# A list scheduler's price for a GpSimd step, and the place of a reload in the DMA queue

## The chip, the cores and the metric

The kernel runs on one core of a Trainium2 chip. The metric is device time in microseconds (us) of one execution, the median of several runs. A second figure, the span, runs from the first to the last instruction of one profiled execution.

## The reference

One mixer layer over 2048 positions of width 1024, all in float32. Two groups of heads share one input projection; what matters here is group B, gated DeltaNet with 8 heads of width 128 in chunks of 64 positions:

```python
xn = rmsnorm(h, norm_w[i]);  proj = einsum('bsd,de->bse', xn, w_in[i])
...
A = where(strict, einsum('bhnik,bhnjk->bhnij', k_beta, k) * L, 0.0)
T = triangular_solve(A + eye, eye, left_side=True, lower=True, unit_diagonal=True)
u = einsum('bhnij,bhnjv->bhniv', T, v * beta[..., None])
w = einsum('bhnij,bhnjk->bhnik', T, k_beta * exp(decay)[..., None])
...
def step(state, inp):                       # scan over the chunks of a head
    v_new = u_c - w_c @ state
    o_c = q_c @ state + qk_c @ v_new
    state = state * a_c + k_c.T @ v_new
```

So each chunk needs a 64x64 unit lower triangular system solved, and each head then needs a recurrence over its chunks. Group A (a gated MLP over blocks of 128 positions), the output projection, a gate with an embedding of its own and a last RMSNorm follow in the same program.

## The kernel before

**Passes and units.** The 2048 positions are worked through in two passes of 1024. In each pass TensorE first does four units of the projection for group A (`v_unit`), then for each of the 8 heads three units: `kq_unit` (keys and queries), `vu_unit` (values), `zz_unit` (gates). A unit is four projections of 24 matmuls each (`proj`, two halves `b` of 512 positions by two blocks of columns). After both passes come the output projection (`out_stream`, PSUM tile `pso`) and the gate (`pg`).

**The order of the work.** The kernel writes its instructions in an order that a list scheduler (`class Flow`, L31) makes while the program is built. Its clock `fl.t` advances by a price for each matmul; `fl.clk` holds a clock for VectorE, ScalarE and GpSimd, advanced by a price for each instruction (`act` L134, `tt` L147, `gtt` L178, `asel` L182, `power` L174 and others). The stream of projections runs until a gate is shut; tasks (`fl.spawn`) wake at the times that they name and put their instructions between the matmuls of the stream. On the chip each engine then executes its instructions strictly in the written order and waits at semaphores. All DMAs are issued by the SP queue, in the written order as well. So a price in `Flow` is not a time on the chip; it decides which instruction stands before which.

**A head's path.** `front` (L719) makes the 64x64 systems of one half of a head in `AT` and writes them to DRAM (`atd`, L780). When both halves are written, `inverse` (L811) solves the 16 systems of the head on GpSimd: it loads `xs` (the identity, from `xinit`, L815) and pieces of `atd` (`ain`, two buffers, L822), waits 4500 ns of the scheduler's time, and then does 63 columns, each with two `gtt` instructions, a product into `xtmp` (L833) and a subtraction from `xs` (L835). At the end it writes `xs` to DRAM (`td`, L841), waits 2600 ns, waits for the chain of the head before (`done`), loads the two diagonal halves of `Dt` (L848) and spawns `chain`. `chain` (L851) is the recurrence: eight steps, each a row of small matmuls into `pc` and `po` with VectorE and ScalarE work between; the second matmul of a step needs `Dt`. Four steps make a half; then the buffer of keys and queries of that half (`kq`) is given back at L907, and `finish` (L919) takes a power on GpSimd (`sso`) and writes `ysc`.

**Gates that matter.** `inverse` of a head starts when its systems are written and when `inverted` has an entry for the head before (L812). `kq_unit` needs one of four `kq` buffers for each half (L672); each head holds two until its chain has given them back, so half `b` of head h+2 waits for half `b` of the chain of head h. At the end of each pass `refill` (L970) stages the next stationary operands through `kq`, `acc` and `pre` buffers too.

Of the kernel before, what the change touches and what calls it, by code (L numbers as in the profile page):

```python
# [106 lines left out]
def trunk(tc, a, out):  # L107
# [7 lines left out]
    fl = Flow()  # L115

    def width(ap):
        return int(np.prod(ap.shape[1:]))

    def mm(o, lhsT, rhs, start, stop):  # L120
        nc.tensor.matmul(o, lhsT, rhs, start=start, stop=stop)  # L121
        n = width(rhs)
        fl.t += max(109.0, 4 + 0.4453 * n) if lhsT.dtype == F32R else max(222.0, 1.7 * n)
        return fl.t + 220
# [9 lines left out]
    def act(o, i, func, after=None, **kw):  # L134
        nc.scalar.activation(o, i, func, **kw)  # L135
        c = 60 + 0.85 * width(i) + (93 if "accum_out" in kw else 0)
        if local(i):
            c += 35
        if not isinstance(kw.get("scale", 1.0), float):
            c += 100  # L140
        t = TABLES.get(func)
        if t and t != fl.table:
            fl.table = t
            c += 1290
        return fl.op("act", c, after)

    def tt(o, x, y, op, after=None):  # L147
        nc.vector.tensor_tensor(o, x, y, op)  # L148
        return fl.op("dve", 76 + 1.04 * width(o), after, local(x, y))

    def stt(o, x, sc, y, op0, op1, after=None):
        nc.vector.scalar_tensor_tensor(o, x, sc, y, op0, op1)  # L152
        return fl.op("dve", (76 if isinstance(sc, float) else 135) + 1.04 * width(o), after, local(x, y))

    def ts(o, x, s1, s2, op0, op1=None, after=None):
        if op1 is None:
            nc.vector.tensor_scalar(o, x, s1, s2, op0)
        else:
            nc.vector.tensor_scalar(o, x, s1, s2, op0, op1)  # L159
        w = width(o)  # L160
        c = 70 + 0.7 * w
        if not isinstance(s1, float):
            c = 135 + (2.6 if op1 is not None else 1.04) * w
        return fl.op("dve", c, after, local(x))
# [12 lines left out]

    def gtt(o, x, y, op, after=None):  # L178
        nc.gpsimd.tensor_tensor(o, x, y, op)  # L179
        return fl.op("pool", 330 + 1.6 * width(o), after)  # L180

    def asel(o, x, after=None):  # L182
        nc.gpsimd.affine_select(o, x, [[0, 4], [1, P]], ALU.is_ge, 0.0, 0, -1)
# [2 lines left out]
    with ExitStack() as outer:  # L186
# [12 lines left out]
        def bank(tag, name, shape=(P, 4, P)):  # L199
            return pp.tile(list(shape), F32, tag=tag, bufs=2 if tag in ("pj", "tr", "m") else 1, name=name)  # L200
# [29 lines left out]
        def gt(tag, name, shape, bufs, dt=F32):  # L230
            return gp.tile(list(shape), dt, tag=tag, bufs=bufs, name=name)
# [487 lines left out]
        def front(p, h, b, st):  # L719
# [64 lines left out]
            if b == 1:  # L784
                fl.spawn(inverse(p, h, st), 2500, 1)
# [25 lines left out]
        def inverse(p, h, st):  # L811
            while 2 * len(inverted) < st["i"]:  # L812
                yield fl.t + 300
            xs = gt("xs", "xs", [P, 8, 64], 1)
            dma(xs, a["xinit"])  # L815
            tmp = gt("xtmp", "xtmp", [P, 160], 1)
            asys = st["atd"].rearrange("b u d j i -> (b u d) (j i)")
            ains = {}

            def load(jc):  # L820
                ains[jc] = gt("ain", "ain", [P, 8, 64], 2)
                dma(ains[jc].rearrange("p j i -> p (j i)"),  # L822
                    asys[None, :, jc * 512:(jc + 1) * 512].to_broadcast([8, 16, 512]))
            load(0)
            load(1)
            yield fl.t + 4500
            for j in range(63):
                if j % 2 == 0:
                    yield from fl.room("pool", 500)
                jc, jj = divmod(j, 8)  # L830
                n, kk = 63 - j, j // 8 + 1
                t_ = tmp[:, :kk * n].rearrange("p (k n) -> p k n", k=kk)
                gtt(t_, ains[jc][:, jj, None, j + 1:].to_broadcast([P, kk, n]),  # L833
                    xs[:, :kk, j:j + 1].to_broadcast([P, kk, n]), ALU.mult)
                f = gtt(xs[:, :kk, j + 1:], xs[:, :kk, j + 1:], t_, ALU.subtract)  # L835
                if jj == 7 and jc < 6:
                    yield f
                    load(jc + 2)
            yield f
            td = dp.tile([64, 16, 64], F32, tag="td", bufs=2, name="td")  # L840
            dma(td.rearrange("(k c) s i -> (c s) k i", c=8), xs)  # L841
            inverted.append(1)
            yield fl.t + 2600
            while len(done) < st["i"]:
                yield fl.t + 300
            for d in range(2):
                dd = slice(d * 64, d * 64 + 64)
                dma(Dt[dd, :, dd], td.rearrange("c (u d) i -> d c u i", d=2)[d])  # L848
            fl.spawn(chain(p, h, st), 4500, 0)

        def chain(p, h, st):  # L851
            beta, gh, gl, ex, ne = SC[p]
            while len(done) < st["i"] or len(st["R"]) < 2:
                yield fl.t + 300
            Sp = state[:, h, :]
            outs = []
            for b in range(2):
                kq, kd, vn, AT, QK, bn, qe = st["B"][b]
                yield from fl.take("ot")
                ot = gt("ot", "ot", [P, 4, P], 1)  # L860
                sso = gt("sso", "sso", [P, 4], 2)
                for u in range(4):
                    c = h * 8 + b * 4 + u
                    cu = slice(c, c + 1)
                    first = p + b + u == 0
                    last = b == 1 and u == 3
                    pc = bank("ch", "pc")
                    if first:
                        r = vn[:, u]
                    else:  # L870
                        yield mm(pc[:, 0], kq[:, u, 0, :], Sp, True, True)
                        r = gt("r", "r", [P, P], 1)
                        yield stt(r, pc[:, 0], ne[:, cu], vn[:, u], ALU.mult, ALU.add)
                    f = mm(pc[:, 1], Dt[:, b * 4 + u], r, True, True)
                    while outs[-1:] == [0]:
                        yield fl.t + 100
                    po = bank("o", "po", [P, 2, P])
                    if not first:
                        mm(po[:, 0], kq[:, u, 1, :], Sp, True, True)
                    yield f  # L880
                    yield act(x1[0:64], pc[0:64, 1], AF.Copy)
                    f = mm(pc[:, 2], AT[:, u], x1, True, True)
                    if not first:
                        act(ot[:, u], po[:, 0], AF.Copy, scale=ex[:, 0, cu])
                    yield f
                    yield tt(r[64:128], r[64:128], pc[64:128, 2], ALU.subtract)
                    yield mm(pc[:, 1], Dt[:, b * 4 + u], r, True, True)
                    w = gt("w", "w", [P, P], 1)
                    yield ts(w, pc[:, 1], bn[:, u:u + 1], None, ALU.mult)
                    more = not (last and p == NPASS - 1)  # L890
                    if more:
                        f = mm(pc[:, 3], kd[:, u], w, True, True)
                    fo = mm(po[:, 1], QK[:, u], w, True, True)
                    outs.append(0)
                    fl.spawn(gather(ot[:, u], po[:, 1], sso[:, u:u + 1], first, outs), fo - fl.t, 0)
                    if more:
                        yield f
                        Sn = state[:, h, :] if last else gt("S", "S", [P, P], 2)
                        if first:
                            f = vcopy(Sn, pc[:, 3])  # L900
                        else:
                            f = stt(Sn, Sp, ex[:, 2, cu], pc[:, 3], ALU.mult, ALU.add)
                        Sp = Sn
                        yield f
                while outs[-1] == 0:
                    yield fl.t + 100
                fl.give("kq")  # L907
                fl.spawn(finish(p, h, b, st, ot, sso, qe, outs[-1]), 0, 1)

        def gather(o, po, ss, first, outs):  # L910
            i = len(outs) - 1
            if first:
                yield vcopy(o, po)
            else:
                yield tt(o, o, po, ALU.add)
            junk = gt("junk", "junkc", [P, P], 2, BF16)
            outs[i] = act(junk, o, AF.Square, accum_out=ss)
# [349 lines left out]
        done, fronts, inverted, SC, mixed, stored, vdone, prepped, Ls = [[] for _ in range(9)]  # L1267
# [114 lines left out]
```

## Time and profile before

| what | value |
|---|---|
| median of 3 runs | 2332.24 us (2331.82 to 2336.56) |
| the profiled execution, its own time | 2334.43 us |
| its span | 2332.7 us |
| mean granted TensorE clock over the span | 0.985 of full |
| busy share: TensorE, VectorE, GpSimd, ScalarE | 96%, 55%, 49%, 43% |

The busy shares are means over the span; GpSimd has little to do outside the two passes of heads. The profiled execution is 2.2 us above the median, and 1.7 us of its time lies outside the span.

### The profile page before, as it was taken

To read this page: it belongs to the slowest core of one execution; us is meant where nothing else is said; L and a number is where in the kernel's file an instruction comes from. 1 tells how busy PE (TensorE), PEld (TensorE's weight loads), DVE (VectorE), ACT (ScalarE), POOL (GpSimd) and SP (SyncE) were. 2 spreads that over 40 slices of the span, in tenths; PEclk is the share of its full clock that TensorE was granted. 3 is DMA by queue.
4 is the path that set the end of the run, shared out by engine and by line. 5 is a ranking of instruction groups with operands and counts; after the bars stand their busy time and mean duration, and the time that the engine had idled before them with its cause. 6 is when DMAs were issued, how large, how long until landed. Compare 5 with 4: busy or idle time off the path is not lost.

```text
span 2332.7 us, 34766 instructions
## 1 busy us (share of the span) xinstructions
PE 2250.4 (96%) x11884; PEld 1878.9 (81%) x11884; DVE 1293.3 (55%) x2845; ACT 999.1 (43%) x2398; POOL 1131.6 (49%) x2246
## 2 busy tenths in 40 slices
PE   8999899999999999999899999999989999999998
PEld 8988688787787779987788878778778878878886
DVE  5465375574665755347466566575664243346665
ACT  5554354453444443445345454454432232244443
POOL 1118668586686772137768668668660000001111
PEclk9999999999999999999999999999999999999999
DMA  5632232323222243222332332232453466452221
GB/s 185 228 117 88 73 99 79 98 72 101 89 87 80 79 148 114 77 76 80 89 98 80 96 99 78 87 87 85 126 167 121 150 200 194 139 185 74 79 77 63
DMA packets 249201, 253.22 MB, mean 109 GB/s; under 512 B 66112, under 2 KB 163904, under 8 KB 249024
## 3 DMA queue, kind: packets, MB, share of 16 engines
q1 hardware_dynamic: 249024, 251.01, 34.6%
q8 instruction: 93, 1.52, 0.3%
q14 instruction: 84, 0.69, 0.1%
HBM read 195.89 MB, written 55.05 MB: 108 GB/s over the span
## 4 chain that ended last, share of the span: by engine, by line
PE 78%; POOL 11%; DMA 5%; issue 2%; DVE 2%; ACT 1%; SPq 1%; POOLq 0%; DVEq 0%; ACTq 0%
PE pj L121 36%; PE pso L121 13%; PE pg L121 7%; PE pc L121 6%; PE pv L121 6%; POOL xs L179 5%; POOL xtmp L179 4%; DMA Dt<-td 2%; PE po L121 2%; PE pe L121 2%; PE pkq L121 1%; DMA wo<-in_wo 1%; DMA td<-xs 1%; PE pm L121 1%; PE ph L127 1%
## 5 line engine op out<-in xcount | busy, mean ns | idle before, releaser
L179 POOL TENSOR_TENSOR xtmp<-ain,xs 128x132 f32<-128x132 f32 (+47 forms) x1008 | 462.4, 459 | 250.9 <-DMA ain<-atd 180.4
L179 POOL TENSOR_TENSOR xs<-xs,xtmp 128x132 f32<-128x132 f32 (+47 forms) x1008 | 483.2, 479 | 79.0
L175 POOL TENSOR_TENSOR rstd<-rstd,nhalf 128x1 f32<-128x1 f32 x64 | 45.8, 722 | 577.3 <-DVE rstd L159 290.3
L121 PE MATMUL pj<-xlo,whi 128*128 128x512 f32 x768 | 315.3, 411 | 0.0
L121 PE MATMUL pj<-xhi,wlo 128*128 128x512 f32 x768 | 314.9, 410 | 0.0
L121 PE MATMUL pj<-xhi,whi 128*128 128x512 f32 x768 | 314.2, 409 | 0.0
L121 PE MATMUL pj<-xrhi,whi 128*128 128x512 f32 x768 | 313.2, 408 | 0.0
L121 PE MATMUL pj<-xrhi,wlo 128*128 128x512 f32 x768 | 312.3, 407 | 0.0
L121 PE MATMUL pj<-xrlo,whi 128*128 128x512 f32 x768 | 311.0, 405 | 0.0
L152 DVE SCALAR_TENSOR_TENSOR acc<-pre,cw,acc 128x512 f32<-128x512 f32 x288 | 227.8, 791 | 23.9 <-ACT acc L135 19.4
L121 PE MATMUL pso<-wolo,yhi 128*128 128x512 f32 x512 | 204.9, 400 | 2.3 <-DVE wolo L148 2.2
L121 PE MATMUL pso<-wohi,ylo 128*128 128x512 f32 x512 | 205.3, 401 | 0.0
L121 PE MATMUL pso<-wohi,yhi 128*128 128x512 f32 x512 | 202.5, 395 | 0.0
L148 DVE TENSOR_TENSOR wlo<-raw,whi 128x512 fp32r<-128x512 f32 x224 | 163.9, 734 | 62.5 <-ACT whi L135 61.6
L135 ACT ACTIVATE whi<-raw 128x512 fp32r<-128x512 f32 x224 | 140.3, 629 | 95.2 <-PE pj L121 71.0
L135 ACT ACTIVATE yhi<-yraw 128x512 fp32r<-128x512 f32 x128 | 80.3, 630 | 215.3 <-PE pso L121 208.6
L121 PEld LDWEIGHTS pj<-xlo,whi 128*128 128x128 f32 x768 | 147.2, 192 | 24.3
L121 PEld LDWEIGHTS pj<-xhi,wlo 128*128 128x128 f32 x768 | 147.0, 191 | 23.9
L121 PEld LDWEIGHTS pj<-xhi,whi 128*128 128x128 f32 x768 | 146.9, 191 | 23.7
L121 PEld LDWEIGHTS pj<-xrhi,wlo 128*128 128x128 f32 x768 | 145.7, 190 | 25.1
L121 PEld LDWEIGHTS pj<-xrlo,whi 128*128 128x128 f32 x768 | 146.0, 190 | 24.5
L148 DVE TENSOR_TENSOR ylo<-yraw,yhi 128x512 fp32r<-128x512 f32 x128 | 89.5, 701 | 135.9 <-ACT yhi L135 133.2
(202 smaller groups left out, 4858.3 us busy)
## 6 DMA issues: line engine op xcount, KB each, us to landing
raw<-in_wu SPq DMA_DIRECT2D x224, 256.0 KB
ain<-atd SPq DMA_DIRECT2D x128, 256.0 KB
yraw<-ysc SPq DMA_DIRECT2D x128, 256.0 KB
vsc<-gv SPq DMA_DIRECT2D x64, 128.0 KB
gn<-vsc SPq DMA_DIRECT2D x32, 256.0 KB
ysc<-gn SPq DMA_DIRECT2D x32, 256.0 KB
ysc<-zb SPq DMA_DIRECT2D x32, 256.0 KB
wo<-in_wo SPq DMA_DIRECT2D x32, 256.0 KB
```

The source lines that it names most:

```text
L121: nc.tensor.matmul(o, lhsT, rhs, start=start, stop=stop)
L127: nc.tensor.transpose(o, i, ident)
L135: nc.scalar.activation(o, i, func, **kw)
L148: nc.vector.tensor_tensor(o, x, y, op)
L152: nc.vector.scalar_tensor_tensor(o, x, sc, y, op0, op1)
L175: nc.gpsimd.tensor_tensor(o, x, y, ALU.pow)
L179: nc.gpsimd.tensor_tensor(o, x, y, op)
```

## The change

Three numbers of the scheduler and the place of one line change. The price of a `gtt` instruction rises from 330 + 1.6 ns per column to 375 + 1.95 ns per column. The entry in `inverted`, which lets the next head's `inverse` issue its loads of `xs` and `ain`, is made after the two loads of `Dt` are issued, no longer right after the write of `td`. The chain is spawned 5000 ns after the loads of `Dt` in place of 4500. No instruction is added or removed; their order changes.

```diff
     def gtt(o, x, y, op, after=None):
         nc.gpsimd.tensor_tensor(o, x, y, op)
-        return fl.op("pool", 330 + 1.6 * width(o), after)
+        return fl.op("pool", 375 + 1.95 * width(o), after)
...
             dma(td.rearrange("(k c) s i -> (c s) k i", c=8), xs)
-            inverted.append(1)
             yield fl.t + 2600
             while len(done) < st["i"]:
                 yield fl.t + 300
             for d in range(2):
                 dd = slice(d * 64, d * 64 + 64)
                 dma(Dt[dd, :, dd], td.rearrange("c (u d) i -> d c u i", d=2)[d])
-            fl.spawn(chain(p, h, st), 4500, 0)
+            inverted.append(1)
+            fl.spawn(chain(p, h, st), 5000, 0)
```

## Rows read from the trace of the kernel before

**Rows 1.** The page, its first part: busy us (share) x instructions of each engine.

```profile
PE 2250.4 (96%) x11884; PEld 1878.9 (81%) x11884; DVE 1293.3 (55%) x2845; ACT 999.1 (43%) x2398; POOL 1131.6 (49%) x2246
```

**Rows 2.** Waits of TensorE over the span: total us, times, longest us.

```profile
PE pc L121 <- DMA Dt<-td: 53.7, 15, 9.5
```

**Rows 3.** The same view, stretches 1100 to 1130 and 1460 to 1500.

```profile
PE pc L121 <- DMA Dt<-td: 8.1, 1, 8.1
...
PE pc L121 <- DMA Dt<-td: 2.2, 1, 2.2
```

**Rows 4.** GpSimd by line, 1378 to 1470: busy us, mean ns | idle before, releaser.

```profile
L179 POOL TENSOR_TENSOR xs<-xs,xtmp 128x56 f32<-128x56 f32 (+47 forms) x63 | 30.1, 478 | 4.9
L179 POOL TENSOR_TENSOR xtmp<-ain,xs 128x56 f32<-128x56 f32 (+47 forms) x63 | 29.1, 463 | 14.7 <-DMA ain<-atd 10.3
L175 POOL TENSOR_TENSOR sso<-sso,nhalf 128x4 f32<-128x4 f32 x2 | 2.1, 1058 | 4.1 <-DVE pre L167 2.2 <-DVE sso L152 1.9
```

**Rows 5.** Timeline of GpSimd: start us, duration us, the instruction [idle before, releaser].

```profile
1383.86 0.29 POOL L179 TENSOR_TENSOR xtmp<-ain,xs 128x63 f32<-128x63 f32 x1 [10.33 <-DMA ain<-atd]
...
1475.07 0.29 POOL L179 TENSOR_TENSOR xtmp<-ain,xs 128x63 f32<-128x63 f32 x1 [10.15 <-DMA ain<-atd]
```

**Rows 6.** Timeline of the SP queue, two heads: start us, us of issuing.

```profile
1101.78 0.38 SPq L841 DMA_DIRECT2D td<-xs  x1
1104.36 0.33 SPq L815 DMA_DIRECT2D xs<-in_xinit  x1
...
1106.22 1.23 SPq L848 DMA_DIRECT2D Dt<-td  x2
...
1463.98 0.38 SPq L841 DMA_DIRECT2D td<-xs  x1
1466.62 1.22 SPq L848 DMA_DIRECT2D Dt<-td  x2
...
1469.24 0.59 SPq L815 DMA_DIRECT2D xs<-in_xinit  x1
1470.75 1.27 SPq L822 DMA_DIRECT2D ain<-atd  x2
```

**Rows 7.** The chain that ended last, the same two heads: start us, us, what.

```profile
1106.82 7.32 DMA Dt<-td
...
1467.21 2.91 DMA Dt<-td
```

**Rows 8.** Timeline of ScalarE: end of a chain, then query half 0 of a later head.

```profile
306.13 0.31 ACT L135 ACTIVATE junkc<-ot 128x128 bf16<-128x128 f32 x1 [2.61 <-DVE ot L148]
308.90 0.58 ACT L135 ACTIVATE pre<-pj 128x512 f32<-128x512 f32 x1
...
390.25 0.31 ACT L135 ACTIVATE junkc<-ot 128x128 bf16<-128x128 f32 x1 [3.45 <-DVE ot L148]
399.79 0.60 ACT L135 ACTIVATE pre<-pj 128x512 f32<-128x512 f32 x1 [0.63 <-PE pj L121]
...
583.13 0.30 ACT L135 ACTIVATE junkc<-ot 128x128 bf16<-128x128 f32 x1
587.25 0.60 ACT L135 ACTIVATE pre<-pj 128x512 f32<-128x512 f32 x1 [0.79 <-PE pj L121]
...
1164.25 0.31 ACT L135 ACTIVATE junkc<-ot 128x128 bf16<-128x128 f32 x1
1166.45 0.60 ACT L135 ACTIVATE pre<-pj 128x512 f32<-128x512 f32 x1 [1.28 <-PE pj L121]
...
1428.82 0.31 ACT L135 ACTIVATE junkc<-ot 128x128 bf16<-128x128 f32 x1 [4.51 <-DVE ot L148]
1436.39 0.60 ACT L135 ACTIVATE pre<-pj 128x512 f32<-128x512 f32 x1 [0.42 <-PE pj L121]
```

**Rows 9.** Stretches: length, busy us (x) of PE, PEld, DVE, ACT, POOL; clock; DMA.

```profile
258.00:262.00 4.00, 4.00 (x13) 3.33 (x12) 1.45 (x4) 0.75 (x2) 3.37 (x9) 0.50 0.14 36
...
1113.50:1117.00 3.50, 2.73 (x10) 2.47 (x11) 0.21 (x1) 0.64 (x2) 2.87 (x9) 0.50 1.08 345
```

## The prediction

> **What bounds the kernel now.** I read the page first. TensorE is busy 96% of the span, 2250.4 of 2332.7 us [rows 1], so what a change of order can win is bounded by the 82 us in which TensorE is idle, and by what its clock loses. The view of waits names the owner of that time: 53.7 us in 15 waits is one thing, a chain matmul that waits for `Dt` [rows 2]. The reader is to see that 15 of the 16 heads pay, that the longest pays 9.5 us, and that it differs by place: an early head of a pass pays 8.1, a settled one 2.2 [rows 3].
>
> Why is `Dt` late? The groups of GpSimd by line and its timeline answer, over one settled head. The 63 products and 63 subtractions are busy 30.1 + 29.1 us, with small gaps of 4.9 + (14.7 - 10.3) us between them: 68.5 us [rows 4]. The scheduler's old price for the same 126 steps is 126 x 330 ns + 1.6 ns x 12,768 columns = 62.0 us (12,768 is twice the sum over the 63 columns of (j//8 + 1)(63 - j)). So the scheduler believes that the inverse ends 6.5 us before it does, writes the chain's matmuls too early into TensorE's order, and TensorE, which executes in order, stands there.
>
> The last view is the SP queue. In a settled head `Dt` is already issued ahead of the next head's `xs` and `ain`; only at the first head of the pass does `xs` go first [rows 6]. There `Dt` shares the DMA engines with those loads, and the chain shows it landing after 7.32 us where a settled head takes 2.91 [rows 7].
>
> **The price of a step.** The new price is 126 x 375 ns + 1.95 ns x 12,768 = 72.1 us: 10.1 us above the old one and 3.6 us above the 68.5 measured. With 500 ns more before the chain, each chain is written 10.6 us later against the stream of projections. The longest wait is 9.5 us [rows 2], so all 15 waits for `Dt` should go: -53.7 us.
>
> After such a wait the clock is low: granted at 0.50, the 1.2 GHz level, while TensorE is busy for 4.00 us in one stretch and 2.73 us in another [rows 9]. At half speed these two lose 2.0 and 1.4 us of work, and the way up again adds about 1 each. For the two long waits and half of that for the four of middle length I take -8 us; the bounds are 0 and twice that.
>
> The Trainium skill ("TensorE: Matmul & The Clock Gate", Part 1) says that the throttled state is the default and that activity releases it. These rows agree: 0.50 follows the wait. By that rule a pause that is moved and still broken up by chain matmuls might keep the clock; the sum below would then end 6 us lower. No row here shows such a pause.
>
> **What the later chain runs into.** The buffers `kq` are next. Half 1 of head h+2 may begin its projection only when half 1 of head h has ended its chain. On ScalarE, `junkc` marks the chain's last step and the second `pre` of a head (query, half 0) the moment at which half 1 begins. I read the slack between the two: 2.8 us for chain 0 of pass 0, 9.5 for chain 1, 4.1 for chain 3, then 2.2 for chain 0 of pass 1 and 7.6 for a settled one, of which there are four alike [rows 8]. The other three of the twelve gates have more than 10.6. A chain 10.6 us later overruns them by 7.8, 1.1, 6.5, 8.4 and four times 3.0 us: 35.8 us. While the gate is shut the scheduler has only the chain's own small matmuls to write, so TensorE stands idle for that time on the chip as well. Two things that I leave out pull against each other: a stall shifts the stream, which gives the next chain slack, and the second head of a pass starts its inverse later by more than 10 us, because it now waits for the first one's end. Following the gates by hand with both gives 35.1 us, so I keep +35.8, with bounds of 0 (no gate shuts) and 64 (the slack is read 3 us too large, because the scheduler's own end of a chain lies behind the row; all gates with less than 13.6 us are overrun).
>
> Three of these stalls are as long as the waits at which the clock fell, so I give back most of that: +6 us, bounds 0 and 9. At the end of each pass `refill` takes `kq` buffers and is released later by the same chain; the stream still has a unit of matmuls to write there, so I take +1 us for both passes, with 0 and 10 as bounds.
>
> **Does GpSimd still keep pace?** The loop of a settled head is 1475.07 - 1383.86 = 91.2 us [rows 5]; less the wait of 2.2 [rows 3], TensorE needs 89.0. GpSimd's steps with 4.1 us of waits for `sso` among them [rows 4] are hidden only as long as its loop stays below that. In the scheduler's own clock the new loop is 72.1 + 9.5 (six selects, four powers) + 2.6 + 0.3 + 4.5 = 89.1 us: as long as TensorE's. That is near enough to add nothing to the stalls, which already stretch the loop; it is the thinnest cover of this sum.
>
> **The entry moved behind `Dt`.** Moved are one load of `xs` and two of `ain`, all on SP, behind two issues of `Dt`. A settled head already has this order [rows 6], so nothing changes there. For the first heads `Dt` lands about 4.4 us sooner (7.32 - 2.91 [rows 7]), inside the wait that the price has removed already, and the next inverse starts about 1.2 us later, the time of two issues [rows 6]. I cost it at 0; the cover is the 10.6 us. If the order is needed there after all, it is worth up to 9 us over two passes. Behind the moved loads on SP stand the loads of weights, four buffers ahead.
>
> **The sum.** -53.7 - 8 + 35.8 + 6 + 1 = -18.9 us. The profiled execution's own time of 2334.43 becomes 2315.5; as that one is 2.2 us above the median of the runs, the predicted median is 2332.24 - 18.9 = 2313.3, say 2313. The likeliest case's own range, by the bounds of its parts taken a third of the way, is 2296 to 2328.
>
> **Rivals.**
> *The waits go and nothing comes back.* The gates overlap with work that I have counted as idle. For it: most of the twelve gates are overrun by 3 us or less. Against it: the two first heads have less than 3 us of slack. Time: 2332.24 - 53.7 - 8 = 2270.5; half of it with half the stalls, 2290.
> *GpSimd's loop is the bound, and the time stays.* For it: the loop of 91.2 us is a ring: `Dt`, chain, `sso` on GpSimd, the rest of the next inverse, `Dt`. If that ring sets the pace, TensorE's order only moves the wait to another matmul. Against it: 4.1 us of the ring are waits that come from the old order, and 91.2 - 4.1 = 87.1 is below 89.0. Time: 2332. It decides when the steps become slower by 1.9 us a head, 15 ns each of 126.
> The Trainium skill ("GPSIMD Engine Reference", section 8, Key points) says that GpSimd shares its SBUF interfaces with VectorE and suffers from VectorE instructions with two SBUF inputs. By that rule a denser VectorE makes the steps longer and the new price nearer the truth; no run here shows by how much.
> *Slower: the `kq` gate costs more than the waits did.* One mechanism: the slack is overstated. With 3 us less at each gate the stalls are 64 us and the clock loses 9, so 2332.24 - 61.7 + 73 = 2343.5. It decides from about 2 us of overstatement on. For it: two first heads with 2.8 and 2.2 us are nearly at the gate already. Against it: the settled heads show a steady 7.6.
>
> **How the numbers follow.** Chances: the forecast 0.45, nothing comes back 0.20, the ring holds the time 0.15, slower 0.20. A measurement of this kernel tells about 0.2% (4.7 us) from no change. Of the forecast's 0.45 nearly all is faster, and a little of the third rival's; so faster 0.65, same 0.15, slower 0.20. The range that leaves out no more than 2 in 10 goes from halfway between 2270 and 2290 to just short of the slower case: 2281 to 2341.
>
> **What would show it.** In the changed kernel: the wait of `pc` for `Dt` falls from 53.7 us to below 10 (the price works); new idle time of TensorE, some 30 us, lies ahead of chain matmuls that wait for VectorE or ScalarE (`r`, `w`, `x`, `S`), just before a key half 1, largest at the third head of each pass (the `kq` gate); `xs` and `ain` stand behind `Dt` at every head; a settled loop of about 90 us in place of 91.2. I am wrong if waits for `Dt` stay above 25 us (the ring), if TensorE's idle time falls by more than 45 us (no gate), or if it grows.

## The result and the profile after

The changed kernel takes 2387.0 us (median of 4 runs, 2383.6 to 2390.7) against 2333.3 before on the same chip: a ratio of 1.0228, 95% interval 1.0209 to 1.0248. It is 54 us slower, where 19 us faster was forecast. The span of the profiled execution grows from 2332.7 to 2385.0 us.

The waits for `Dt` are gone, 0.8 us in place of 53.7 [rows 2]. In their place TensorE waits, in many pieces, for VectorE inside the chain: 66 us in the four lines below. The waits of TensorE over the span, in total us, times, longest us, and the line of the page on its busy time:

```profile
PE pc L121 <- DVE r L152: 27.8, 17, 7.2
PE pc L121 <- DVE vn L148: 17.1, 6, 3.7
PE pc L121 <- DVE r L148: 11.3, 19, 2.0
PE pc L121 <- DVE w L157: 10.2, 15, 1.2
...
PE pc L121 <- DMA Dt<-td: 0.8, 1, 0.8
```

```profile
PE 2280.2 (96%) x11884; PEld 1894.2 (79%) x11884; DVE 1312.8 (55%) x2845; ACT 990.6 (42%) x2387; POOL 1132.0 (47%) x2246
```

TensorE's busy time rose too, from 2250.4 [rows 1], with the same 11,884 instructions; its mean clock fell from 0.985 to 0.980. So of the 52.3 us by which the span grew, 29.8 are busy time and 22.5 idle time: chain matmuls that run alone count as busy, and idle time alone understates the loss. (ScalarE shows 11 instructions fewer than before; in the two traces all 11 are `ACT_TABLE_LOAD`.) The loop of a settled head has grown: on GpSimd's timeline, from the first column of one inverse to the next,

```profile
1416.32 0.29 POOL L179 TENSOR_TENSOR xtmp<-ain,xs 128x63 f32<-128x63 f32 x1 [9.99 <-DMA ain<-atd]
...
1438.86 1.01 POOL L175 TENSOR_TENSOR sso<-sso,nhalf 128x4 f32<-128x4 f32 x1 [6.96 <-DVE sso L152]
...
1513.39 0.29 POOL L179 TENSOR_TENSOR xtmp<-ain,xs 128x63 f32<-128x63 f32 x1 [9.83 <-DMA ain<-atd]
```

That is 97.1 us, where it was 91.2 [rows 5]; the mean of the seven loops of the second pass went from 90.6 to 95.1 us. `sso`, which is a product of the chain, comes 7 us after GpSimd is ready for it in this loop. The steps themselves have not changed: in the group view of this loop,

```profile
L179 POOL TENSOR_TENSOR xtmp<-ain,xs 128x56 f32<-128x56 f32 (+47 forms) x63 | 30.1, 477 | 14.3 <-DMA ain<-atd 10.0
L179 POOL TENSOR_TENSOR xs<-xs,xtmp 128x56 f32<-128x56 f32 (+47 forms) x63 | 29.0, 460 | 4.9
```

30.1 + 29.0 us busy and 4.3 + 4.9 between, 68.3 us against 68.5 [rows 4].

**The first place of the loss: the `kq` gate.** On ScalarE, the query of half 0 (the moment at which half 1 wants its buffer), the end of the chain two heads back, and the first `pre` of half 1, behind its first 24 matmuls:

```profile
1561.42 0.58 ACT L135 ACTIVATE pre<-pj 128x512 f32<-128x512 f32 x1
...
1572.07 0.31 ACT L135 ACTIVATE junkc<-ot 128x128 bf16<-128x128 f32 x1 [2.33 <-DVE ot L148]
1581.99 0.60 ACT L135 ACTIVATE pre<-pj 128x512 f32<-128x512 f32 x1 [1.15 <-PE pj L121]
```

The chain ends 10.7 us after half 1 could have begun; before, it ended 7.6 us ahead of that in a settled head [rows 8]. This is the longest of the settled heads. Read in the same way, half 1 is late at 11 of the 12 gates, and the stretches without a projection matmul (`pj`) there are 16.6 and 13.9 us at the third head of each pass and 1.0 to 11.5 elsewhere, 76 us in all; in the kernel before none is over 0.7 us. TensorE's timeline in this one holds no `pj` from 1561 to 1572.8, only the chain's steps with their latency and a few small matmuls of other tasks:

```profile
1563.37 0.49 PE L121 MATMUL pc<-r,Dt 128*128 128x128 f32 x2 [0.94 <-DVE r L148]
1564.65 0.49 PE L121 MATMUL pc<-w,kd 128*128 128x128 f32 x2 [0.79 <-DVE w L157]
...
1567.39 0.49 PE L121 MATMUL pc<-r,Dt 128*128 128x128 f32 x2 [1.32 <-DVE r L152]
...
1569.78 0.63 PE L121 MATMUL pc<-r,Dt 128*128 128x128 f32 x2 [1.06 <-DVE r L148]
1570.95 0.77 PE L121 MATMUL po<-w,QK 128*128 128x128 f32 x2 [0.54 <-DVE w L157]
...
1572.80 0.63 PE L121 MATMUL pj<-xrhi,whi 128*128 128x512 f32 x1
```

```profile
1562.00:1570.00 8.00, 3.75 (x24) 2.78 (x23) 7.29 (x18) 3.75 (x16) 7.21 (x12) 1.00 0.17 63
1570.00:1576.00 6.00, 5.46 (x18) 4.52 (x18) 2.84 (x8) 1.03 (x3) 4.50 (x9) 0.50 0.17 46
```

The second fence is that stretch in the view of windows (columns as in [rows 9]): over the first 8 us TensorE is busy for 3.75 at the full clock; then the clock is granted at 0.50, the 1.2 GHz level, for the next 6, although TensorE had never stood idle for more than 1.3 us at a time. The `pj` at 1572.80 is a long 0.63 us.

**The second place: a memset of `ws`.** A `zz` unit begins by loading `ws` (L642) and clearing a corner of it on VectorE (L643). The SP queue, then VectorE, at one settled head (the load of `Dt` is L847 in the changed kernel):

```profile
1406.35 0.38 SPq L841 DMA_DIRECT2D td<-xs  x1
1409.12 1.21 SPq L847 DMA_DIRECT2D Dt<-td  x2
1410.38 0.61 SPq L815 DMA_DIRECT2D xs<-in_xinit  x1
1411.10 1.26 SPq L822 DMA_DIRECT2D ain<-atd  x2
1412.40 0.45 SPq L642 DMA_DIRECT2D ws<-in_ws  x1
```

```profile
1411.58 0.69 DVE L148 TENSOR_TENSOR wlo<-raw,whi 128x512 fp32r<-128x512 f32 x1 [0.70 <-ACT whi L135]
1418.20 0.11 DVE L643 MEMSET ws<- 64x64 f32 x1 [5.93 <-DMA ws<-in_ws]
1418.34 0.35 DVE L152 SCALAR_TENSOR_TENSOR r<-pc,ne,vn 128x128 f32<-128x128 f32 x1
```

SP waits for `td` to land and comes to its next issue 2.8 us after `td`; it issues five loads, and only then `ws`, which takes 5.7 us to land. VectorE stands 5.9 us at the memset, and the first `r` of the chain is queued right behind it; TensorE's `pc` then waits 3.7 us for that `r`:

```profile
1418.75 0.49 PE L121 MATMUL pc<-r,Dt 128*128 128x128 f32 x2 [3.71 <-DVE r L152]
```

Over the span, in VectorE's waits:

```profile
DVE ws L643 <- DMA ws<-in_ws: 74.9, 12, 8.7
```

In the kernel before the same line is 5.3 us in 2 waits. The load stood behind `ain` there too, but VectorE came to the memset 12 us after it was issued:

```profile
1472.07 0.46 SPq L642 DMA_DIRECT2D ws<-in_ws  x1
...
1484.29 0.11 DVE L643 MEMSET ws<- 64x64 f32 x1
```

**The ends of the passes.** The stretch from the last projection of pass 0 to the first one of pass 1, and the one from the output projection to the end, before and then after:

```profile
862.20:981.70 119.50, 115.89 (x930) 112.80 (x929) 60.72 (x154) 51.54 (x113) 32.78 (x65) 0.99 0.35 110
1701.40:2332.70 631.30, 614.66 (x2771) 496.85 (x2769) 306.26 (x540) 213.23 (x449) 67.26 (x108) 0.99 0.41 132
...
865.00:997.10 132.10, 125.89 (x973) 120.60 (x972) 65.85 (x170) 52.95 (x123) 44.60 (x90) 0.95 0.33 101
1744.90:2385.00 640.10, 622.14 (x2802) 503.62 (x2800) 309.97 (x552) 215.06 (x459) 74.69 (x125) 0.99 0.41 130
```

They grew by 12.6 and 8.8 us, the heads of pass 0 by 3 and those of pass 1 by 28. Not all of the 21 us is new work lost: the two stretches also hold 74 more matmuls, most of them of chains, which stood inside the passes before.

### The profile page after: what moved, and what is told of

It is laid out like the page before. It is cut to its first block, busy times and chain, and to the rows that moved or that the text cites. A ratio compares the mean times of both kernels' runs of the same rounds, so it can differ in the third digit from the quotient of the medians.

```text
span 2385.0 us, 34725 instructions
## 1 busy us (share of the span) xinstructions
PE 2280.2 (96%) x11884; PEld 1894.2 (79%) x11884; DVE 1312.8 (55%) x2845; ACT 990.6 (42%) x2387; POOL 1132.0 (47%) x2246
## 4 chain that ended last, share of the span: by engine, by line
PE 78%; DMA 6%; DVE 5%; POOL 5%; SPq 2%; issue 2%; ACT 1%; DVEq 0%; POOLq 0%; ACTq 0%
PE pj L121 35%; PE pso L121 13%; PE pg L121 7%; PE pv L121 6%; PE pc L121 6%; DMA ws<-in_ws 3%; POOL xtmp L179 2%; POOL xs L179 2%; PE po L121 2%; PE pe L121 2%; PE pkq L121 2%; PE pm L121 1%; DVE acc L152 1%; DMA td<-xs 1%; DMA wo<-in_wo 1%
## 5 line engine op out<-in xcount | busy, mean ns | idle before, releaser
L179 POOL TENSOR_TENSOR xtmp<-ain,xs 128x132 f32<-128x132 f32 (+47 forms) x1008 | 471.4, 468 | 238.5 <-DMA ain<-atd 169.6
L179 POOL TENSOR_TENSOR xs<-xs,xtmp 128x132 f32<-128x132 f32 (+47 forms) x1008 | 478.1, 474 | 79.0
L121 PEld LDWEIGHTS pj<-xrhi,whi 128*128 128x128 f32 x768 | 146.6, 191 | 24.8
```

## The experiments

All times are medians; ratios are to the kernel before, measured beside each run, with 95% intervals.

**The price alone** (old place of the entry, 4500 ns):

```diff
-        return fl.op("pool", 330 + 1.6 * width(o), after)
+        return fl.op("pool", 375 + 1.95 * width(o), after)
```

> Before, with the new price of a GpSimd step alone; the entry in inverted and the 4500 ns stay as they were. Theory G (the stream stands at the kq gate because chains are written later): the gates still shut, but less, since the next inverse may be released before the loads of Dt; 2350 to 2375 us. Rival Q (the moved loads are the harm, the price is harmless or good): at or below the kernel before, 2280 to 2333 us. Rival S (the price does all of it): as the changed kernel, 2380 to 2390 us.

2423.3 us, 1.0392 (1.0375 to 1.0409). All three expectations missed: it is 36 us slower than the whole change. The SP queue of a settled head shows why; waits of TensorE and VectorE follow:

```profile
1345.47 0.38 SPq L841 DMA_DIRECT2D td<-xs  x1
1348.06 0.34 SPq L815 DMA_DIRECT2D xs<-in_xinit  x1
1348.50 1.34 SPq L822 DMA_DIRECT2D ain<-atd  x2
1349.94 1.23 SPq L848 DMA_DIRECT2D Dt<-td  x2
```

```profile
PE pc L121 <- DMA Dt<-td: 46.8, 8, 7.8
PE pc L121 <- DVE r L152: 40.3, 13, 7.6
```

```profile
DVE ws L643 <- DMA ws<-in_ws: 83.6, 11, 8.7
```

With the longer price an inverse ends, in the scheduler's order, behind the next head's `atd`, so the next `xs` and `ain` are released at once and stand ahead of `Dt`. What only the first head of a pass showed before [rows 6] now happens in a settled head too. So the moved entry, with the 500 ns, earns 36 us here: it repairs something that the price breaks.

**The moved entry alone:**

```diff
-            inverted.append(1)
             yield fl.t + 2600
...
+            inverted.append(1)
             fl.spawn(chain(p, h, st), 4500, 0)
```

> Before, with the entry in inverted moved behind the loads of Dt alone; old price, 4500 ns. Theory G: no gate shuts, and Dt of the first head of each pass lands some 4 us sooner: 2322 to 2331 us, waits for Dt 40 to 50 us in place of 53.7. Rival Q: every head pays the later loads, about 2.6 us each: 2350 us or more.

2322.8 us, 0.9958 (0.9944 to 0.9972): 10.6 us faster, within theory G's range; the waits for `Dt` end a little below it. The first head of the second pass now waits 2.1 us for `Dt` (stretch 1090 to 1130) where it waited 8.1 [rows 3], and the total is

```profile
PE pc L121 <- DMA Dt<-td: 39.1, 16, 4.7
```

**The chain later, without the price:**

```diff
-            fl.spawn(chain(p, h, st), 4500, 0)
+            fl.spawn(chain(p, h, st), 15100, 0)
```

> Before, with the chain spawned 15100 ns after the loads of Dt in place of 4500 (10.6 us later, as in the changed kernel), old price, old place of the entry: the chain comes later, the inverses are no longer in the scheduler's clock. Theory G: waits for Dt near 0, TensorE idle at the kq gate instead; 2335 to 2370 us. Rival R (only the longer inverses in the scheduler's ring do harm): the waits for Dt go and nothing comes back, 2270 to 2300 us.

2328.9 us, 0.9985 (0.9975 to 0.9994), a little better than my range. No wait for `Dt` is left in this trace; most of the time comes back at the `kq` gate, where the stretches without `pj` add to about 39 us. Smaller waits for `r`, `w` and GpSimd's selects, and the memset, are in the lines below. So the lateness of the chain by itself is a trade at par: 4.5 us better, where the prediction's sum, which prices the loop at nothing, says 19. The 54 us come from what the price does besides.

```profile
PE pc L121 <- DVE r L148: 11.1, 13, 2.5
PE pd L121 <- POOL R L183: 8.6, 6, 3.5
```

```profile
DVE ws L643 <- DMA ws<-in_ws: 36.9, 9, 9.6
```

**Six `kq` buffers,** in the changed kernel and, as a control, in the kernel before (`kd` shares the buffers of `vn`, so a separate `kd` is left out; some first loads of `x` take buffers of `AT` and `QK` in its place, and three more requests for `kq` rise to 6):

```diff
-CAPS = {..., "kq": 4, ...}
+CAPS = {..., "kq": 6, ...}
...
-                kq = gt("kq", "kq", [P, 4, 2, P], 4)
+                kq = gt("kq", "kq", [P, 4, 2, P], 6)
...
-            kd = gt("kd", "kd", [P, 4, P], 4)
             vn = gt("vn", "vn", [P, 4, P], 4)
+            kd = vn
```

> The changed kernel with six kq buffers in place of four. To make room, the decayed keys kd share the buffers of vn, so the state's update uses wrong operands: this leaves out a separate kd; the instructions and their number stay. Theory G: the gate never shuts, waits for Dt stay near 0, 2280 to 2315 us, faster than before. Rival R (the ring through GpSimd, 96 us a head, sets the pace whatever the buffers): 2370 us or more.

> The control of the run with six kq buffers: the same six buffers (kd shares the buffers of vn, so the state's update uses wrong operands) with the old price, the old place of the entry and 4500 ns. Theory G: the gate does not shut in the kernel before, so six buffers bring nothing there, the waits for Dt stay near 53 us, 2325 to 2340 us. Rival: the buffers or the missing kd themselves win the time, 2280 to 2300 us.

Changed kernel with six buffers: 2282.8 us, 0.9785 (0.9771 to 0.9800), 104 us below the changed kernel with four. Kernel before with six: 2334.5 us, 1.0011 (0.9999 to 1.0022), nothing. So the `kq` buffers carry the loss, at the gate and, since `refill` takes them too, at the ends of the passes; without it the whole change is worth 50 us. Here the chains drift later from head to head, from 14 us behind the start of half 1 at the third head to 41 and 46 at the last of a pass, and the stream does not wait for them: no stretch without `pj` at these gates is over 1.3 us. The waits, of TensorE for `Dt` and of VectorE at the memset, with six buffers and the new price:

```profile
PE pc L121 <- DMA Dt<-td: 5.1, 2, 4.2
```

```profile
DVE ws L643 <- DMA ws<-in_ws: 5.8, 4, 2.0
```

**The scheduler's loop 4 us shorter, the chain as late:**

```diff
-            yield fl.t + 4500
+            yield fl.t + 500
             for j in range(63):
...
-            fl.spawn(chain(p, h, st), 5000, 0)
+            fl.spawn(chain(p, h, st), 9000, 0)
```

> The changed kernel with the scheduler's wait ahead of the first column of an inverse cut from 4500 to 500 ns and the chain spawned 9000 ns after Dt in place of 5000, so that a chain is as late as before against its inverse's loads while the scheduler's GpSimd loop is 4 us shorter. Theory L (the loop of GpSimd in the scheduler's clock, longer than TensorE's, is what shuts the gate at every head): most gates open again, 2325 to 2355 us. Rival (the lateness of 10.6 us alone shuts them): 2375 to 2395 us.

2372.0 us, 1.0171 (1.0148 to 1.0194): between both expectations, 15 us better than the changed kernel. The loop matters, but something else stood in the way: the wait at the memset had grown to 81.6 us. The edit also puts `td` and `Dt` 4 us earlier in the written order; no run holds that apart.

**The memset of `ws` moved to where `ws` is used,** in the changed kernel and, as a control, in the kernel before:

```diff
             mv, rs = norms
+            nc.vector.memset(ws[64:128, 0:64], 0.0)
...
             dma(ws, a["ws"][h])
-            nc.vector.memset(ws[64:128, 0:64], 0.0)
```

> The changed kernel with the VectorE memset of ws (L643) issued at the start of mix, where ws is used, and not at the start of a zz unit; the scheduler's order of all else is the same. Theory W (VectorE stands at this memset because the load of ws lies behind td, Dt, xs and ain in the SP queue, 74.9 us in 12 waits, and the chain behind it): that wait goes and 30 to 60 us with it, 2325 to 2357 us. Rival (the memset only waits where VectorE had nothing to do, and the kq gates are the whole loss): 2375 us or more.

> The control: the kernel before with the memset of ws issued at the start of mix. There it waits 5.3 us in 2 waits. Theory W: 2327 to 2334 us, within 0.3% of before. Rival (the place of the memset matters for another reason): below 2320 or above 2340 us.

Changed kernel: 2359.6 us, 1.0112 (1.0098 to 1.0125), 27 us below the changed kernel, a little slower than theory W's range. Before: 2330.3 us, 0.9986 (0.9976 to 0.9996). So the place of the memset is half of the loss; 75 us of waiting on VectorE were worth 27 us of time.

**Both, the shorter loop and the moved memset:**

> The changed kernel with the shorter scheduler's wait before an inverse (500 ns) and the chain 9000 ns after Dt, as in the earlier run, and with the memset of ws at the start of mix. Its memset waited 81.6 us there. Theory W and L together (the two losses add up: the memset's wait, and gates shut by the scheduler's GpSimd loop): 2325 to 2350 us, at least 8 us below the changed kernel with the memset moved alone (2359.6). Rival (the loop does not matter once the memset is out of the way): 2355 us or more.

2332.0 us, 0.9980 (0.9966 to 0.9993): 27.6 us below the changed kernel with the memset moved alone. With these two losses out, the changed price is level with the kernel before and with the later chain alone (2328.9). It is no gain: 2.6 us of waits for `Dt` are left, but what they cost comes back, as it did there, at the gate, where the stretches without `pj` add to about 48 us.

**Smaller steps.** The entry moved, old price, and the chain 2.5 us later (`4500` to `7000`); and the entry moved with a price of 350 + 1.75 ns and 4500:

> Old price, the entry moved behind Dt, the chain spawned 7000 ns after Dt in place of 4500: 2.5 us later, about the wait of a settled head, less than its slack of 7.6. Theory G: the waits for Dt fall from 39 us to below 15 and no gate shuts but the first of each pass; 2296 to 2312 us. Rival R (the ring through GpSimd holds the pace of 91 us): within 5 us of the 2323 us of the moved entry alone.

> The entry moved behind Dt, 4500 ns, and a price of 350 + 1.75 ns per column, 66.4 us for the 126 steps, near the 68.5 us measured. Theory G: the gates of the first heads shut for some 12 us, the settled ones stay open, waits for Dt below 10 us; 2300 to 2325 us. Rival (any longer price does harm): above 2340 us.

2305.5 us, 0.9887 (0.9869 to 0.9905), and 2317.3 us, 0.9942 (0.9926 to 0.9959), both times within theory G's ranges. With 7000 ns the waits for `Dt` are 12.3 us, as it said; with the price of 350 + 1.75 ns they are not below 10:

```profile
PE pc L121 <- DMA Dt<-td: 21.3, 14, 3.3
```

A delay of 2.5 us is inside the slack of 7.6 us of a settled head [rows 8]. A price close to the measured 68.5 us is worse than the old one with a small delay; against the moved entry alone (0.9958) it is 5 us better, with intervals that overlap.

**The fastest:** the version with 7000 ns and the memset moved:

> The version with the old price, the moved entry and 7000 ns, with the memset of ws issued at the start of mix. Its memset waits 31.1 us in 8 waits. Theory W: 8 to 25 us less, 2280 to 2298 us, the fastest of all that keep the reference's work. Rival: 2300 to 2308 us.

2290.8 us, 0.9817 (0.9803 to 0.9830): 42 us faster than before, with the clock at 0.996 of full. What is left of the waits for `Dt`:

```profile
PE pc L121 <- DMA Dt<-td: 13.5, 8, 2.9
```

## Why the prediction was wrong

**The waits for `Dt`: right.** -53.7 us were forecast; 0.8 us are left. The steps of GpSimd stay at 68.3 us, with VectorE busy for 59% of the loop where it was 60%. The Trainium skill ("GPSIMD Engine Reference", section 8, Key points) says that GpSimd shares its SBUF interfaces with VectorE; no run here shows what that costs.

**The `kq` gate: the mechanism right, the size wrong.** I had +35.8; the stretches without `pj` at the gates add to 76 us in the changed kernel. For the lateness alone, in the run with 15100 ns, they add to about 39, near the sum, but partly by luck: the third heads have 13 and 17 us where I had 7.8 and 8.4, the others together about 8 where I had 19.6. (Four gates, not three, had more than 10.6 us of slack; the sum is the same.) The term missing from the changed kernel is the next one.

**"That is near enough to add nothing to the stalls": the step that failed.** I added up the scheduler's GpSimd loop as 89.1 us, set it equal to TensorE's 89.0, and priced it at nothing. Both numbers were wrong for the purpose. The scheduler's own clock, read off while the program is written (its prices, not times of the chip), gives:

```
                                   kq gate shut,   loop of inverses,   staging at the
                                   us in all       median, pass 1      ends of passes, us
before                              0.0            88.0                 2.2
changed                            81.5            91.3                22.9
changed, 500 ns and 9000 ns        52.9            89.4                20.1
later chain alone (15100 ns)       42.0            89.2                15.5
changed, six kq buffers             0.0            91.8                 0.0
```

The new loop is 2 us longer than I had it, because GpSimd's entries in that clock do not follow each other without gaps. And 89.0 was read on the chip: in the scheduler's clock the stream needs 88.0 a head, the pace of the kernel before, whose inverses hardly wait for each other. In the changed kernel 13 of the 16 inverses are ready and wait 2.8 to 12.5 us for the one before. So the loop of inverses sets the pace of the written order, the chains stay late, and the `kq` gate shuts at every head from the third on, on the chip at 11 of 12. With six buffers the loop is as long and does no harm (2282.8 us): it costs only through the buffers. On the chip the loop shortened by 4 us is worth 27.6 us (2359.6 to 2332.0). I had called this the thinnest cover of the sum, and gave it no price in the likeliest case.

**The ends of the passes: +1 us, too small.** The scheduler's staging gates, which wait for what `refill` brings through the `kq` buffers, grew by 21 us, and by 13 with the later chain alone, against bounds of 0 and 10. On the chip the two stretches grew by 21 us, part of it chain matmuls that only moved there. With what the memset waits in that run, 36.9 us in all, this is a likely reason why the later chain alone won 4.5 us and not 19; no run tells the two apart.

**"Behind the moved loads on SP stand the loads of weights": incomplete.** Between them stand the loads of `ws` and `bs`, and VectorE's memset waits for the first. In a settled head `ws` was issued behind `ain` before as well, but VectorE reached the memset only 12 us later. The later chain brings `td`, the start of the `zz` unit and the first `r` together. The step should have named who waits for every load behind the moved ones; it cost 27 us.

**"I cost it at 0" for the moved entry: wrong both ways.** Alone it wins 10.6 us; on top of the price, with the 500 ns, 36. I read from [rows 6] that a settled head has the new order already, and did not ask whether the price would change that.

**The clock.** I took 8 us for the waits that go and gave 6 back, 2 us won. The clock has two levels, 0.50 and 1.00, so a mean of 0.985 over 2332.7 us is about 70 us at the lower one, and 0.980 over 2385.0 about 95. By that estimate the clock costs some 12 us more than before, not 2 less. In the stretch shown above it fell at 1570 us after 8 us of broken-up chain matmuls. By the rule of the Trainium skill ("TensorE: Matmul & The Clock Gate", Part 1) that activity releases the throttled state, I allowed that chain matmuls in a pause might keep the clock; the 0.50 in that stretch shows that here they did not.

**The rivals.** Slower had 0.20, by an overstated slack. The sign was right, and 2343.5 was too small by 43 us, because the cause is the loop and the memset. "Nothing comes back", 2270.5, is near what six buffers show: 2282.8. The ring rival named the right loop in the wrong clock: on the chip GpSimd does not hold the pace, as six buffers show; in the scheduler's clock it does. Of the signs of being wrong that I named, the last one came: TensorE's idle time grew, from 82.3 to 104.8 us.

## What to carry to other kernels

A price in a list scheduler acts in two ways: it places the consumer, and it lengthens the producer's loop in the scheduler's clock. If that loop is near the one that it hides behind, move the consumer alone, by no more than the wait that the trace shows; here 2.5 us did what 10.6 could not. A buffer gate sets the price of being late: read its slack before moving anything, at the first trips as well as the settled ones, and compare the two loops in the same clock. When a DMA is moved in a queue that issues in the written order, follow every later load in it to the instruction that waits for it, however small: a memset of 0.11 us held VectorE for 75 us in all.

## What the runs showed of the hardware

In the changed kernel, from 1562 to 1570 us, TensorE ran short matmuls at the full clock, busy for 3.75 us of 8 and never idle for more than 1.33 us at a time. Then the clock was granted at 0.50 for the next 6 us, of which it was busy for 5.46. I had allowed that it might hold.

A load can be late without being large: `ws` landed 11.8 us after SP had come to `td` (1406.35 to 1418.14 us), about 6 of them before its own issue.
